# All token chunks routed ahead of the fused expert stage, whose freed memory holds more gather rows and a third weight pair; low halves later; tiles at 64 bytes

## The chip, the cores and the metric

One core of a Trainium2 chip runs the whole program. The metric is device time in microseconds (us) of one execution. PE is the matrix engine, DVE, ACT and POOL are the vector, scalar and GpSimd engines, SP is the engine whose queue issues most DMAs here. Each engine works through its own instructions in order; the program's order on each engine is set before it runs.

## What is computed

Two layers on x [1, 512, 1024] in fp32. A layer is `x + gate * mixer(h)` and then `x + gate * peer_ffn(h)`, each with `h = rms_norm(x) * (1 + scale) + shift`; shift, scale and gate come from `silu(c) @ w + b` (the modulation). The first layer's mixer is a gated linear recurrence (`rglru_mixer`), the second's is an attention with forget gates (`fox_mixer`). The part that the change is about is the ffn:

```python
def peer_ffn(h, q_w, subkey1, subkey2, expert_u, expert_v):   # per chunk xc of 128 tokens
    q = (xc @ q_w).reshape(128, 8, 2, 128)
    s1, s2 = q[:, :, 0] . subkey1, q[:, :, 1] . subkey2       # 128 keys each
    v1, i1 = top_k(s1, 16);  v2, i2 = top_k(s2, 16)
    top_s, top_c = top_k(v1[:, None] + v2[None, :], 16)       # per head
    expert = i1[top_c // 16] * 128 + i2[top_c % 16]           # of 16384
    g = softmax(top_s)
    act = gelu(expert_u[expert] . xc)
    return sum_k (g * act) * expert_v[expert]
```

## The kernel before

**Products.** A product of fp32 is three matmuls of rounded parts, hi x hi, lo x hi and hi x lo. `split` makes the parts: ACT copies the high half (L191), DVE subtracts it for the low half (L192). For weights these are `whi` and `wlo`. A `Stream` goes through a fixed plan of weight blocks of 512 KB; `fill` (L137) has SP load a pair of blocks (1 MB) into one of two `wraw` buffers and splits each block three ahead of its use. A buffer is free for the next load once DVE has subtracted its second block.

**The ffn (`peer`).** Tokens are four chunks of 128. The first three are computed densely: "expert" in the code is a group c of 128 experts (c = 0..127, those with the same first key), all 128 evaluated for 384 tokens, and weighted with a gate that is zero where the expert was not chosen. The fourth chunk is computed by gathering: for each of a token's 128 choices POOL fetches one row of u (later of v) per token by an indirect DMA of 128 rows, 512 KB (`fetch`, L700), into a ring of four `rows` buffers; DVE multiplies it with the token (L706) or adds it to the sum `accg` (L716).

Stages of `peer`: `queries` (products with the keys, top 16 on DVE); then a first-up stage, in which 56 groups (c < 56) are projected and their GELU stored to `ascr` in DRAM, with a `Background` that computes `route(0..2)` (which experts, from DVE operations on small tables) and `dense_gates(0..2)` (gate tables, stored to `gscr`) in small steps; then the fused stage, in the order c = 56..127 and then 0..55. I call its two parts A and B:

- A: `expert_in` projects the group (24 matmuls of 384 columns, L259 to L261), ACT takes the GELU (L751), DVE multiplies with the gate (L757, from `gtile`, loaded for eight groups at a time, L756), `split` makes `wh` and `wl`; `expert_out` then multiplies with v into six accumulators (18 matmuls of 512 columns, L769).
- B: the same, but the GELU comes back from `ascr` (L753, a ring of three `at2` buffers) instead of a projection.

During it `pump` runs the fourth chunk's generator `gathered` (its `route`, then 128 rows of u, then 128 of v) and some rows of modulation after it. A pump gives credits: 4.6 per group for the first eight, then 3.7 in A and 1.4 in B; a gathered row costs 1.2.

**Modulation rows (`mod_gen`).** Each row is a load of 512 KB by SP (L158) and a product on DVE (L160, L161). They are worked off as background elsewhere: eight rows of `l1_mix` at the end of the first mixer's output projection (the last argument of `lru`) and eight in the first ffn's fused stage (ring of four, that of the gathered rows); 12 in the attention's `during` (the 8 gates of `l1_mix` and 4 of `l1_ffn`'s 24 rows, one buffer) and the other 20 of `l1_ffn` after it.

The order on each engine comes from a scheduler that may move an instruction ahead of others of its engine; pools decide which load waits for which use.

Of the kernel before, what the change touches and what calls it, by code (L numbers as in the profile page):

```python
# [35 lines left out]
PUMP = (3.7, 1.4)  # L36
# [3 lines left out]
M1 = 8  # L40
M2 = 4
# [465 lines left out]
def peer(g, h, u, v, grow_fn, after, nd):  # L507
# [8 lines left out]
    with pool(tc, name="pk", bufs=1) as pk:  # L516
        hn = pk.tile([128, D], F32, name="hn")
        iota_f = iota_row(g, pk, 128, F16, "iota_f")
        iota_e = iota_f.rearrange("p (a b) -> p a b", b=8)
        vals = [pk.tile([128, TC, PH, TOPK], F32, name=f"vals{w}") for w in range(2)]  # L520
        idxs = [pk.tile([128, TC, PH, TOPK], U32, name=f"idxs{w}") for w in range(2)]
        def top16(val, idx, src, n):
            tk = pk.tile([128, 128], F32, name="tk", tag="tk", bufs=4)
# [54 lines left out]
        def route(t):  # L578

            v1, v2 = vals[0][:, t], vals[1][:, t]  # L580
            cand = pk.tile([128, PH, NCAND], F32, name="cand", tag="cand")
# [7 lines left out]
            top = pk.tile([128, PH, TOPK], F32, name="top", tag="top")  # L589
            pos = pk.tile([128, PH, TOPK], U32, name="pos", tag="pos")  # L590
# [11 lines left out]
            shp = [128, TOPK, HK]
            for q in range(2):
# [557 lines left out]
```

## Time and profile before

| | |
|---|---|
| median of 3 runs | 3401.5 us (3399.68 to 3401.56) |
| profiled execution, its own time | 3391.9 us, span 3390.2 us |
| mean granted TensorE clock | 0.973 |
| first ffn: fused A, fused B | 751 to 1393 us, 1393 to 1647 us |
| second ffn: fused A, fused B | 2485 to 3128 us, 3128 to 3385 us |
| DMA | 816.9 MB, 241 GB/s over the span |

The stages are windows of the trace: the first and last matmuls of L769 bound them, and A ends where the last projected group has been multiplied with v. Rows of a timeline read: start, duration, engine, line, operation, out<-in, and in brackets how long the engine had been idle before and what it waited for. Rows of the view of waits read: who waited for whom, us in total, times, longest.

### The profile page before, as it was taken

How to read it: one execution, taken by the hardware profiler on the slowest of the kernel's cores; microseconds unless marked ns; L12 is line 12 of the kernel's file. 1: busy time of each engine (PE TensorE's matmuls, PEld its weight loads, DVE VectorE, ACT ScalarE, POOL GpSimd, SP SyncE). 2: the span in 40 equal slices, each digit the busy share in tenths (PEclk: the TensorE clock that was granted, in tenths of full speed). 3: DMA queues.
4: the chain of work that ended last, by engine and by line, in shares of the span. 5: the costliest groups of instructions: out<-in, count | busy, mean ns of one | idle time of the engine just before them, and what ended most of it. 6: DMA issues, size and time to landing. Idle time of an engine off the chain costs nothing.

```text
span 3390.2 us, 44187 instructions
## 1 busy us (share of the span) xinstructions
PE 3158.9 (93%) x16256; PEld 2712.4 (80%) x16256; DVE 2647.0 (78%) x5245; ACT 1482.6 (44%) x2065; POOL 790.7 (23%) x672
## 2 busy tenths in 40 slices
PE   5987999999999999999999989999999999999999
PEld 4875889988888888777777767889988888887777
DVE  7867889876777787877679777799867777788775
ACT  4872237863333333333458723257843333332332
POOL 0000000003544454441000000000025454444430
PEclk9998999999999999999999989999999999999999
DMA  6445235778888889988441152336879888899994
GB/s 255 149 146 178 103 126 197 257 273 288 315 299 315 322 322 329 351 310 324 141 153 58 49 192 92 114 133 245 283 250 323 320 302 314 321 330 331 325 335 169
DMA packets 300762, 816.91 MB, mean 241 GB/s; under 512 B 24320, under 2 KB 153344, under 8 KB 272000
## 3 DMA queue, kind: packets, MB, share of 16 engines
q1 hardware_dynamic: 197312, 453.85, 38.6%
q0 software_dynamic: 75008, 269.00, 21.8%
q10 hardware_dynamic: 28224, 91.24, 6.9%
q8 instruction: 127, 2.08, 0.2%
q14 instruction: 91, 0.75, 0.1%
HBM read 733.00 MB, written 81.00 MB: 240 GB/s over the span
## 4 chain that ended last, share of the span: by engine, by line
issue 23%; PE 23%; DVE 19%; DMA 17%; POOL 10%; ACT 7%; SPq 0%; ACTq 0%; POOLq 0%; DVEq 0%
POOL rows L700 10%; DMA at<-ascr 6%; DMA rows<-in_l_v_dram,ei 6%; PE pacc L259 4%; DVE wlo L192 4%; PE pacc L260 4%; PE pacc L261 4%; PE vacc L769 2%; DVE accg L716 2%; PE gps L683 2%; DMA mw<-in_l_ffn_mw_dram 2%; DMA mw<-in_l_mix_mw_dram 1%; DVE mw L160 1%; ACT st L685 1%; ACT whi L191 1%
## 5 line engine op out<-in xcount | busy, mean ns | idle before, releaser
L191 ACT ACTIVATE whi<-wraw 128x1024 fp32r<-128x1024 f32 (+2 forms) x646 | 663.1, 1035 | 740.2 <-PE pacc L260 314.4
L261 PE MATMUL pacc<-hhi,wlo 128*128 128x384 f32 (+1 forms) x2632 | 935.4, 355 | 39.9 <-DVE wlo L192 39.9
L259 PE MATMUL pacc<-hhi,whi 128*128 128x384 f32 (+1 forms) x2632 | 930.6, 354 | 15.9 <-ACT at L751 14.4
L260 PE MATMUL pacc<-hlo,whi 128*128 128x384 f32 (+1 forms) x2632 | 930.0, 353 | 0.0
L192 DVE TENSOR_TENSOR wlo<-wraw,whi 128x1024 fp32r<-128x1024 f32 (+2 forms) x646 | 767.7, 1194 | 171.8 <-ACT whi L191 169.5
L769 PE MATMUL vacc<-whi,wh 128*128 128x512 f32 x1536 | 613.8, 400 | 23.6 <-ACT wh L191 23.4
L700 POOL DMA_INDIRECT rows<-in_l_u_dram,ei x256 | 370.1, 1446 | 1127.5 <-DMA wraw<-in_l_uT_dram 716.7
L769 PE MATMUL vacc<-wlo,wh 128*128 128x512 f32 x1536 | 612.9, 399 | 20.7 <-DVE wlo L192 20.5
L769 PE MATMUL vacc<-whi,wl 128*128 128x512 f32 x1536 | 612.1, 399 | 5.7 <-DVE wl L192 5.5
L261 PEld LDWEIGHTS pacc<-hhi,wlo 128*128 128x128 f32 x2632 | 502.7, 191 | 71.2 <-DVE wlo L192 49.8
L259 PEld LDWEIGHTS pacc<-hhi,whi 128*128 128x128 f32 x2632 | 503.1, 191 | 49.4 <-ACT at L751 16.6
L260 PEld LDWEIGHTS pacc<-hlo,whi 128*128 128x128 f32 x2632 | 502.2, 191 | 29.2 <-issue 2.4
L191 ACT ACTIVATE wh<-at 128x384 fp32r<-128x384 f32 x256 | 133.8, 524 | 806.4 <-DVE at L757 789.3
L700 POOL DMA_INDIRECT rows<-in_l_v_dram,ei x256 | 377.2, 1474 | 454.6 <-DVE accg L716 396.9
L706 DVE SCALAR_TENSOR_TENSOR rows<-rows,hn 128x1024 f32<-128x1024 f32 x256 | 304.6, 1221 | 130.3 <-DMA rows<-in_l_u_dram,ei 130.1
L769 PEld LDWEIGHTS vacc<-wlo,wh 128*128 128x128 f32 x1536 | 290.4, 189 | 94.6 <-DVE wlo L192 30.9
L769 PEld LDWEIGHTS vacc<-whi,wh 128*128 128x128 f32 x1536 | 290.7, 189 | 93.7 <-ACT wh L191 30.9
L769 PEld LDWEIGHTS vacc<-whi,wl 128*128 128x128 f32 x1536 | 290.7, 189 | 85.3 <-DVE wl L192 16.3
L716 DVE SCALAR_TENSOR_TENSOR accg<-rows,act,accg 128x1024 f32<-128x1024 f32 x254 | 325.5, 1282 | 41.0 <-DMA rows<-in_l_v_dram,ei 38.4
L757 DVE TENSOR_TENSOR at<-at,gtile 128x384 f32<-128x384 f32 x256 | 140.6, 553 | 108.4 <-DMA at<-ascr 105.9
L685 ACT ACTIVATE st<-gps 128x512 f32<-128x512 f32 x192 | 185.3, 1117 | 47.6 <-PE gps L683 45.2
L192 DVE TENSOR_TENSOR wl<-at,wh 128x384 fp32r<-128x384 f32 x256 | 141.3, 554 | 68.8 <-ACT wh L191 68.8
(266 smaller groups left out, 3229.5 us busy)
## 6 DMA issues: line engine op xcount, KB each, us to landing
wraw<-in_l_uT_dram SPq DMA_DIRECT2D x128, 1024.0 KB, 6.4
wraw<-in_l_v_dram SPq DMA_DIRECT2D x128, 1024.0 KB, 8.4
gscr<-st ACTq DMA_DIRECT2D x48, 1024.0 KB, 5.6
gtile<-gscr SPq DMA_DIRECT2D x32, 1536.0 KB, 12.3
mw<-in_l_mix_mw_dram SPq DMA_DIRECT2D x48, 512.0 KB, 6.4
mw<-in_l_ffn_mw_dram SPq DMA_DIRECT2D x48, 512.0 KB, 4.0
ascr<-at ACTq DMA_DIRECT2D x112, 192.0 KB, 4.1
at<-ascr SPq DMA_DIRECT2D x112, 192.0 KB, 5.2
```

Source lines behind the costliest of these rows:

```text
L191: g.nc.scalar.activation(hi, raw, AF.Copy)
L192: g.nc.vector.tensor_sub(lo, raw, hi)
L259: nc.tensor.matmul(ps, whi[:, k, :], hhi[:, k, :n], start=(k == 0), stop=False)
L260: nc.tensor.matmul(ps, whi[:, k, :], hlo[:, k, :n], start=False, stop=False)
L261: nc.tensor.matmul(ps, wlo[:, k, :], hhi[:, k, :n], start=False, stop=(k == KD - 1))
L683: T.matmul(gps[:, r, :], p2[:, tk_, :, :].rearrange("p a b -> p (a b)"), pg[i][:, :, tk_, :], start=(i == 0), stop=(i == 1))
L685: A.activation(st[:, :, q * 4:q * 4 + 4].rearrange("p e t -> p t e"), gps, AF.Copy, scale=1.0 / GSCALE)
L700: nc.gpsimd.indirect_dma_start(out=rows, out_offset=None, in_=src, in_offset=bass.IndirectOffsetOnAxis(ap=ei[:, j:j + 1], axis=0))
L706: V.scalar_tensor_tensor(r, r, 1.0, hn, op0=OP.mult, op1=OP.mult, accum_out=act[:, j:j + 1]))
L716: tc.keep_in_program_order(V.scalar_tensor_tensor(acc, r, w, acc, op0=OP.mult, op1=OP.add))
L757: V.tensor_tensor(at.rearrange("p (b t) -> p b t", t=16), at.rearrange("p (b t) -> p b t", t=16), env["gt"][:, :, c % 8, :], op=OP.mult)
L769: T.matmul(acc[t][d], x[:, ts], y[:, d, :], start=(i == 0 and x is wh and y is vh), stop=(i == PK - 1 and x is wl))
```

## The change

- `route` for the fourth chunk, with the indices `ei`, is computed at the end of the first-up stage's background instead of at the start of the fused stage. Routing's tiles lie in a pool `rt` of their own, which is closed before the fused stage.
- In the memory so freed: eight `rows` buffers instead of four, four `at2` buffers instead of three, and two more `wraw` buffers in the fused stage's pool `vw`, which take every third weight load (`g.stream.third`) until group PK - 16.
- `expert_in` leaves out the subtraction for `wl` and returns it, to be issued after the pump.
- The pump gives 3.5 in A and 1.3 in B, and the first eight groups are no exception.
- The first ffn's fused stage has all 16 first rows of `l1_mix` (ring of eight) and the end of the first mixer none; the attention's `during` has 16 first rows of `l1_ffn` beside the 8 gates, and 8 rows remain after it.
- `pad` puts small tiles into three pools, with a memset on POOL each. `hhi`, `hlo`, `whi`, `wlo`, `wraw` and what lies behind them begin at 0 modulo 64 bytes instead of 32; `wh`, `wl`, `gtile` and `rows` were at 0 and stay there; the attention's own tiles go from 0 to 32.

```diff
@@ -33,12 +33,11 @@
 NEG = -3.0e38
 NFIRST = 56
 NEARLY = 8
-PUMP = (3.7, 1.4)
+PUMP = (3.5, 1.3)
 GP = 4.0
 GSCALE = 32768.0
 M0 = 12
-M1 = 8
-M2 = 4
+M2 = 16
 MB = 1
 LP = 2.0
 
@@ -49,6 +48,11 @@
 
 def pool(tc, **kw):
     return tc.tile_pool(reuse_waits="tile", **kw)
+
+
+def pad(g, pool, size):
+
+    g.nc.gpsimd.memset(pool.tile([128, size // 4], F32, name="pad", bufs=1), 0.0)
 
 
 def bcast_rows(ap, n, length):
@@ -85,6 +89,7 @@
     nc.vector.memset(g.ones, 1.0)
     g.mhalf = g.const.tile([128, 1], F32, name="mhalf")
     nc.vector.memset(g.mhalf, -0.5)
+    pad(g, g.const, 32)
     g.order = range(TC)
 
 
@@ -124,7 +129,8 @@
         self.g, self.ahead = g, ahead
         self.blocks = [(i, b) for i in items for b in range(i[2])]
         self.raw, self.parts = None, []
-        self.n = 0
+        self.n = self.loads = 0
+        self.third = None
 
     def fill(self, last):
 
@@ -133,7 +139,9 @@
         while len(self.parts) <= last:
             (src, shape, n), b = self.blocks[len(self.parts)]
             if b == 0:
-                self.raw = g.wraw.tile([128, n, *shape], F32, name="wraw", tag="wraw")
+                self.loads += 1
+                src_pool = self.third if self.third and self.loads % 3 == 0 else g.wraw
+                self.raw = src_pool.tile([128, n, *shape], F32, name="wraw", tag="wraw")
                 nc.sync.dma_start(self.raw, src)
             raw = self.raw[:, b]
             hi = g.wsp.tile([128, *shape], F32R, name="whi", tag="whi")
@@ -515,12 +523,15 @@
     with pool(tc, name="pk", bufs=1) as pk:
         hn = pk.tile([128, D], F32, name="hn")
-        iota_f = iota_row(g, pk, 128, F16, "iota_f")
+        rguard = pool(tc, name="rt", bufs=1)
+        rt = rguard.__enter__()
+        pad(g, rt, 224)
+        iota_f = iota_row(g, rt, 128, F16, "iota_f")
...
-        thr = pk.tile([128, TOPK, HK], BF, name="thr")
+        thr = rt.tile([128, TOPK, HK], BF, name="thr")
...
-            cand = pk.tile([128, PH, NCAND], F32, name="cand", tag="cand")
+            cand = rt.tile([128, PH, NCAND], F32, name="cand", tag="cand")
...
-            gt = pk.tile([128, PH, TOPK], F32, name="gt", tag="gt_", bufs=3)
+            gt = (rt if t < nd else pk).tile([128, PH, TOPK], F32, name="gt", tag="gt_", bufs=3 if t < nd else 1)
...
             routes[t] = [*e, gt.rearrange("p a b -> p (a b)")]
+            if t >= nd:
+                ei = pk.tile([128, 128], I32, name="ei")
+                V.scalar_tensor_tensor(ei, e[0], float(PK), e[1], op0=OP.mult, op1=OP.add)
+                routes[t].append(ei)
             yield 0.6
@@ -688,10 +703,7 @@
 
         def gathered(t, out):
 
-            yield from route(t)
-            e1, e2, gt = routes[t]
-            ei = pk.tile([128, 128], I32, name="ei")
-            V.scalar_tensor_tensor(ei, e1, float(PK), e2, op0=OP.mult, op1=OP.add)
+            gt, ei = routes[t][2:]
             act = env["vw"].tile([128, 128], F32, name="act", tag="act", bufs=1)
             acc = env["vw"].tile([128, D], F32, name="accg", tag="accg", bufs=1)
 
@@ -729,15 +741,19 @@
             queries(pw, psum)
             natural(g, psum, h, TC - 1, hn)
             grow = grow_fn(psum)
-            bg = Background(*[route(t) for t in range(nd)], *[dense_gates(t, pu, pw, psum) for t in range(nd)])
+            bg = Background(*[route(t) for t in range(nd)], *[dense_gates(t, pu, pw, psum) for t in range(nd)],
+                            *[route(t) for t in range(nd, TC)])
             for c in range(NEARLY, NFIRST):
                 first_up(pw, psum, c)
                 bg.pump(GP)
             bg.finish()
+        rguard.__exit__(None, None, None)
         with pool(tc, name="vw", bufs=2) as vw, pool(tc, name="vps", bufs=1, space=PSUM) as psum:
-            gguard = pool(tc, name="gat", bufs=4)
+            gguard = pool(tc, name="gat", bufs=8)
             gat = gguard.__enter__()
             env["gat"], env["vw"] = gat, vw
+            pad(g, vw, 192)
+            g.stream.third = vw
             bg = Background(*late, *after(gat))
             acc = [[psum.tile([128, 512], F32, name=f"vacc{t}{d}") for d in range(2)] for t in range(nd)]
             order = [*range(NFIRST, PK), *range(NFIRST)]
@@ -746,7 +762,7 @@
             def expert_in(i):
 
                 c = order[i]
-                at = vw.tile([128, ND], F32, name="at2", tag="at2", bufs=3)
+                at = vw.tile([128, ND], F32, name="at2", tag="at2", bufs=4)
                 if c >= NFIRST:
                     A.activation(at, proj_t(g, psum, h, ND), AF.Gelu)
                 else:
@@ -758,8 +774,9 @@
                                 env["gt"][:, :, c % 8, :], op=OP.mult)
                 wh = vw.tile([128, ND], F32R, name="wh", tag="wh", bufs=5)
                 wl = vw.tile([128, ND], F32R, name="wl", tag="wl", bufs=5)
-                split(g, wh, wl, at)
+                A.activation(wh, at, AF.Copy)
                 ready[i] = (wh, wl)
+                return lambda: V.tensor_sub(wl, at, wh)
 
             def expert_out(i, t):
                 wh, wl, vh, vl = ready[i]
@@ -770,25 +787,25 @@
                                  stop=(i == PK - 1 and x is wl))
 
             def pump(i):
-                bg.pump(4.6 if i < 8 else PUMP[0] if order[i] >= NFIRST else PUMP[1])
-
-            expert_in(0)
-            expert_in(1)
+                bg.pump(PUMP[0] if order[i] >= NFIRST else PUMP[1])
+
+            expert_in(0)()
+            expert_in(1)()
             for i in range(0, PK - 4, 2):
+                if i == PK - 16:
+                    g.stream.third = None
                 ready[i] += g.stream.take()
                 ready[i + 1] += g.stream.take()
-                for t in range(nd):
-                    expert_out(i, t)
-                pump(i)
-                expert_in(i + 2)
-                for t in range(nd):
-                    expert_out(i + 1, t)
-                pump(i + 1)
-                expert_in(i + 3)
+                for j in (i, i + 1):
+                    for t in range(nd):
+                        expert_out(j, t)
+                    low = expert_in(j + 2)
+                    pump(j)
+                    low()
             bg.finish()
             gguard.__exit__(None, None, None)
             for i in (PK - 2, PK - 1):
-                expert_in(i)
+                expert_in(i)()
             last = range(PK - 4, PK)
             for i in last:
                 ready[i] += g.stream.take()
@@ -1057,8 +1074,8 @@
         with pool(tc, name="mw0", bufs=8) as mw:
             h = normed("l0_mix", mod=mod("l0_mix", mw, first, 8))
         lru(g, h, *arg("lru_", "conv", "bias", "lam"),
-            lambda p: (mod("l0_mix", p, gate, MB), mod("l0_ffn", p, first[:M0], MB)), grow("l0_mix"), lambda p: (mod("l0_ffn", p, (*first[M0:], *gate)), mod("l1_mix", p, first[:M1])))
-        peer(g, normed("l0_ffn"), flat("l0_u"), flat("l0_v"), grow("l0_ffn"), lambda p: (mod("l1_mix", p, first[M1:], 4),), 3)
+            lambda p: (mod("l0_mix", p, gate, MB), mod("l0_ffn", p, first[:M0], MB)), grow("l0_mix"), lambda p: (mod("l0_ffn", p, (*first[M0:], *gate)),))
+        peer(g, normed("l0_ffn"), flat("l0_u"), flat("l0_v"), grow("l0_ffn"), lambda p: (mod("l1_mix", p, first, 8),), 3)
         fox(g, normed("l1_mix"), *arg("fox_", "fb", "qg", "kg"), lambda p: (mod("l1_mix", p, gate, 1), mod("l1_ffn", p, first[:M2], 1)),
             grow("l1_mix"), lambda p: (mod("l1_ffn", p, (*first[M2:], *gate)),))
         peer(g, normed("l1_ffn"), flat("l1_u"), flat("l1_v"), grow("l1_ffn"), lambda p: (), 3)
```

Where it moves instructions. First DVE in part A of the first layer, once the rows flow (L757 gate multiplication, `wl` and `wlo` low halves, L706 gathered rows). Before:

```order
1273 L757 TENSOR_TENSOR at_7691<-at_7691,gtile 128x384
1274 L192 TENSOR_TENSOR wl<-at_7691,wh 128x384
1275 L192 TENSOR_TENSOR wlo<-wraw,whi 128x1024 x2
1276 L757 TENSOR_TENSOR at_7773<-at_7773,gtile 128x384
1277 L192 TENSOR_TENSOR wl<-at_7773,wh 128x384
1278 L706 SCALAR_TENSOR_TENSOR rows,act<-rows,hn 128x1024 x4
1279 L192 TENSOR_TENSOR wlo<-wraw,whi 128x1024 x2
1280 L757 TENSOR_TENSOR at_7839<-at_7839,gtile 128x384
1281 L192 TENSOR_TENSOR wl<-at_7839,wh 128x384
1282 L192 TENSOR_TENSOR wlo<-wraw,whi 128x1024
1283 L706 SCALAR_TENSOR_TENSOR rows,act<-rows,hn 128x1024 x4
```

The same place after (the lines are now L773, L718, L779 for `wl` and L200 for `wlo`):

```order
1247 L773 TENSOR_TENSOR at_7487<-at_7487,gtile 128x384
1248 L718 SCALAR_TENSOR_TENSOR rows,act<-rows,hn 128x1024 x3
1249 L779 TENSOR_TENSOR wl<-at_7487,wh 128x384
1250 L200 TENSOR_TENSOR wlo<-wraw,whi 128x1024 x2
1251 L773 TENSOR_TENSOR at_7552<-at_7552,gtile 128x384
1252 L718 SCALAR_TENSOR_TENSOR rows,act<-rows,hn 128x1024 x3
1253 L779 TENSOR_TENSOR wl<-at_7552,wh 128x384
1254 L200 TENSOR_TENSOR wlo<-wraw,whi 128x1024 x2
```

Each group now has the multiplication, three rows, `wl` and two `wlo`, where before groups without rows and groups with four alternated and `wl` stood right behind the multiplication.

DVE where the fused stage begins, before (the fold of the fourth chunk's route, L574, and its indices `ei`; behind them the first row):

```order
1245 L757 TENSOR_TENSOR at_7287<-at_7287,gtile 128x384
1246 L757 TENSOR_TENSOR at_7325<-at_7325,gtile 128x384
1247 L192 TENSOR_TENSOR wlo<-wraw,whi 128x1024
1248 L192 TENSOR_TENSOR wl<-at_7287,wh 128x384
1249 L192 TENSOR_TENSOR wl<-at_7325,wh 128x384
1250 L623 TENSOR_TENSOR ge<-j,col 128x1024
1251 L624 TENSOR_TENSOR ge<-ge,tab_7607 128x1024
1252 L574 TENSOR_TENSOR ge<-ge 128x512
1253 L574 TENSOR_TENSOR ge<-ge 128x256
1254 L574 TENSOR_TENSOR ge<-ge 128x128
1255 L576 TENSOR_TENSOR e_7513<-ge 128x64
1256 L694 SCALAR_TENSOR_TENSOR ei<-e_7512,e_7513 128x128
```

And after (L634, L635, L585, L587 are the same operations of the route, L648 `ei`):

```order
1234 L635 TENSOR_TENSOR ge<-ge,tab_7296 128x1024
1235 L200 TENSOR_TENSOR wlo<-wraw,whi 128x1024
1236 L585 TENSOR_TENSOR ge<-ge 128x512
1237 L585 TENSOR_TENSOR ge<-ge 128x256
1238 L585 TENSOR_TENSOR ge<-ge 128x128
1239 L587 TENSOR_TENSOR e_7236<-ge 128x64
1240 L648 SCALAR_TENSOR_TENSOR ei<-e_7235,e_7236 128x128
1241 L773 TENSOR_TENSOR at_7383<-at_7383,gtile 128x384
1242 L779 TENSOR_TENSOR wl<-at_7383,wh 128x384
```

The route's last steps and `ei` have moved ahead of the first multiplication; the route's earlier steps stood ahead of it in both.

SP's queue at the end of the first mixer, before (`lru_out` are its last weights, `qw` and `sk` the ffn's first, `gcol` belongs to the norm between):

```order
53 L137 DMA wraw<-in_l_qw_dram 128x2048
54 L158 DMA mw<-in_l_mix_mw_dram 128x1024 x2
55 L137 DMA wraw<-in_l_sk_dram 128x256
56 L155 DMA mod_b<-in_l_mix_mb_dram 128x24
57 L158 DMA mw<-in_l_mix_mw_dram 128x1024 x5
58 L204 DMA gcol<-in_l_ffn_g_dram 128x8
59 L137 DMA wraw<-in_l_sk_dram 128x256
60 L158 DMA mw<-in_l_mix_mw_dram 128x1024
```

After:

```order
53 L145 DMA wraw<-in_l_qw_dram 128x2048
54 L145 DMA wraw<-in_l_sk_dram 128x256
55 L163 DMA mod_b<-in_l_mix_mb_dram 128x24
56 L212 DMA gcol<-in_l_ffn_g_dram 128x8
57 L145 DMA wraw<-in_l_sk_dram 128x256
```

The eight loads of `l1_mix` rows are gone from there.

More of the change, by code (lines that the diff above doesn't have):

```diff
@@ L517, in peer @@
         hn = pk.tile([128, D], F32, name="hn")
-        iota_f = iota_row(g, pk, 128, F16, "iota_f")
+        rguard = pool(tc, name="rt", bufs=1)
+        rt = rguard.__enter__()
+        pad(g, rt, 224)
+        iota_f = iota_row(g, rt, 128, F16, "iota_f")
         iota_e = iota_f.rearrange("p (a b) -> p a b", b=8)
-        vals = [pk.tile([128, TC, PH, TOPK], F32, name=f"vals{w}") for w in range(2)]
-        idxs = [pk.tile([128, TC, PH, TOPK], U32, name=f"idxs{w}") for w in range(2)]
+        vals = [rt.tile([128, TC, PH, TOPK], F32, name=f"vals{w}") for w in range(2)]
+        idxs = [rt.tile([128, TC, PH, TOPK], U32, name=f"idxs{w}") for w in range(2)]
         def top16(val, idx, src, n):
-            tk = pk.tile([128, 128], F32, name="tk", tag="tk", bufs=4)
+            tk = rt.tile([128, 128], F32, name="tk", tag="tk", bufs=4)
             V.max(val[:, 0:8], src)
@@ L561, in peer @@
         HK = QH * TOPK
-        thr = pk.tile([128, TOPK, HK], BF, name="thr")
-        row = pk.tile([128, TOPK, HK], BF, name="rowlen")
-        col = pk.tile([128, TOPK, HK], BF, name="col")
+        thr = rt.tile([128, TOPK, HK], BF, name="thr")
+        row = rt.tile([128, TOPK, HK], BF, name="rowlen")
+        col = rt.tile([128, TOPK, HK], BF, name="col")
         for i in range(TOPK):
@@ L588, in route @@
             yield 1.5
-            top = pk.tile([128, PH, TOPK], F32, name="top", tag="top")
-            pos = pk.tile([128, PH, TOPK], U32, name="pos", tag="pos")
+            top = rt.tile([128, PH, TOPK], F32, name="top", tag="top")
+            pos = rt.tile([128, PH, TOPK], U32, name="pos", tag="pos")
             for hd in range(PH):
@@ L593, in route @@
                 yield 0.7
-            posb = pk.tile([128, PH * TOPK], BF, name="posb", tag="posb")
+            posb = rt.tile([128, PH * TOPK], BF, name="posb", tag="posb")
             V.tensor_copy(posb, pos.rearrange("p a b -> p (a b)"))
-            f1 = pk.tile([128, PH, TOPK], F32, name="f1", tag="f1")
+            f1 = rt.tile([128, PH, TOPK], F32, name="f1", tag="f1")
             V.tensor_copy(f1, idxs[0][:, t])
-            d1 = pk.tile([128, PH, TOPK], F32, name="d1", tag="d1")
+            d1 = rt.tile([128, PH, TOPK], F32, name="d1", tag="d1")
             V.tensor_copy(d1[:, :, 0:1], f1[:, :, 0:1])
             V.tensor_sub(d1[:, :, 1:], f1[:, :, 1:], f1[:, :, :-1])
-            e = [pk.tile([128, PH * TOPK], F32, name=f"e{w}", tag=f"e{w}", bufs=3) for w in range(2)]
+            e = [rt.tile([128, PH * TOPK], F32, name=f"e{w}", tag=f"e{w}", bufs=3) for w in range(2)]
             shp = [128, TOPK, HK]
@@ L607, in route @@
                 for w, src in enumerate((d1[:, hs], idxs[1][:, t, hs])):
-                    x = pk.tile(shp, BF, name=f"tab{w}", tag=f"tab{w}")
+                    x = rt.tile(shp, BF, name=f"tab{w}", tag=f"tab{w}")
                     A.activation(x.rearrange("p r (h k) -> p r h k", h=QH),
@@ L611, in route @@
                     tab.append(x)
-                ge = pk.tile(shp, BF, name="ge", tag="ge")
-                ge2 = pk.tile(shp, BF, name="ge2", tag="ge2")
+                ge = rt.tile(shp, BF, name="ge", tag="ge")
+                ge2 = rt.tile(shp, BF, name="ge2", tag="ge2")
                 ps_ = posb[:, ks]
@@ L619, in route @@
                 yield 2.6
-                j = pk.tile([128, HK], BF, name="j", tag="j")
+                j = rt.tile([128, HK], BF, name="j", tag="j")
                 fold(ge2, j)
```

2 lines of the change are left out of this document (1 added, 1 removed).

## The prediction, made before the changed kernel had run

> **What bounds the kernel now.** I read the page's busy shares first, then cut the span by stage, then asked in each stage what every engine waits for, and last how fast an undisturbed expert runs.
>
> ```profile
> PE 3158.9 (93%) x16256; PEld 2712.4 (80%) x16256; DVE 2647.0 (78%) x5245; ACT 1482.6 (44%) x2065; POOL 790.7 (23%) x672
> core 0: us, PE busy (x) PEld busy (x) DVE busy (x) ACT busy (x) POOL busy (x), PEclk, DMA share, GB/s
> 751.00:1393.00 642.00, 613.66 (x2976) 543.93 (x2975) 491.39 (x634) 206.47 (x286) 306.61 (x213) 0.98 0.86 311
> 1393.00:1647.00 254.00, 240.73 (x1009) 188.53 (x1008) 192.53 (x263) 85.60 (x114) 69.75 (x46) 0.99 0.87 312
> 2485.00:3128.00 643.00, 610.68 (x2978) 540.73 (x2977) 492.20 (x636) 207.15 (x286) 304.08 (x213) 0.98 0.87 311
> 3128.00:3385.00 257.00, 241.36 (x1008) 189.49 (x1006) 179.66 (x221) 79.95 (x107) 68.18 (x44) 0.99 0.79 283
> ```
>
> The four windows are the two fused stages, each cut into A (72 experts projected on the spot) and B (56 experts read back from `ascr`). They hold 1796 of the span's 3390.2 us, so the price of one expert decides. A quiet expert is read from three GELUs of stage A and eighteen output products of stage B:
>
> ```profile
> 793.64 0.47 ACT L751 ACTIVATE at<-pacc 128x384 f32<-128x384 f32 x1
> ...
> 818.78 0.47 ACT L751 ACTIVATE at<-pacc 128x384 f32<-128x384 f32 x1
> 1427.20 0.40 PE L769 MATMUL vacc<-whi,wh 128*128 128x512 f32 x1
> ...
> 1431.40 0.40 PE L769 MATMUL vacc<-whi,wh 128*128 128x512 f32 x1
> 2014.82 0.39 PE L299 MATMUL oacc<-whi,yhi 128*128 128x512 f32 x1
> ...
> 2018.90 0.39 PE L299 MATMUL oacc<-whi,yhi 128*128 128x512 f32 x1
> ```
>
> Between the GELUs lie three experts: 25.14 / 3 = 8.38 us. Between the two `vacc` rows lie 18 matmuls, all of one expert in B: 4.20 us, 233 ns each. The floors are 72 x 8.38 = 603 and 56 x 4.20 = 235 us; measured are 642, 254, 643 and 257. So 39, 19, 40 and 22 us are lost, 120 in all. What PE, DVE and ACT waited for in the first A, and the later B's waits:
>
> ```profile
> PE pacc L261 <- DVE wlo L192: 17.4, 11, 2.6
> PE vacc L769 <- ACT wh L191: 8.5, 8, 2.3
> DVE rows L706 <- DMA rows<-in_l_u_dram,ei: 65.9, 32, 4.3
> DVE wl L192 <- ACT wh L191: 33.1, 56, 0.6
> DVE wlo L192 <- ACT whi L191: 31.7, 35, 4.0
> DVE accg L716 <- DMA rows<-in_l_v_dram,ei: 16.1, 13, 2.5
> ACT whi L191 <- DMA wraw<-in_l_v_dram: 11.8, 5, 3.5
> ACT whi L191 <- DMA wraw<-in_l_uT_dram: 11.0, 3, 4.4
> SPq L137 <- DVE wlo L192: 551.8, 69, 12.4
> PE vacc L769 <- DVE wlo L192: 10.3, 6, 4.1
> DVE at L757 <- DMA at<-ascr: 60.0, 29, 8.2
> ACT whi L191 <- DMA wraw<-in_l_v_dram: 55.9, 15, 8.2
> SPq L753 <- DVE wl L192: 97.9, 33, 8.6
> ```
>
> In A the DVE is 491.4 us busy and 146.8 waiting by these four rows: 638 of 642. It has no slack, though PE is the busier engine: it works in order, so whatever it waits for delays the weights' low halves (`wlo`), for which PE then waits. It waits longest for gathered rows (82 us), since only four can be in flight; SP's next weight load waits for `wlo` all the while.
>
> **The change, part by part.**
>
> *Stage A: eight rows, low half later, lower pump.* Rows per expert go from 3.7/1.2 = 3.08 to 3.5/1.2 = 2.92. A row occupies DVE 1.15 us from start to start:
>
> ```profile
> 1055.31 1.22 DVE L706 SCALAR_TENSOR_TENSOR rows<-rows,hn 128x1024 f32<-128x1024 f32 x1
> ...
> 1056.45 1.22 DVE L706 SCALAR_TENSOR_TENSOR rows<-rows,hn 128x1024 f32<-128x1024 f32 x1
> ```
>
> So 72 x 0.16 x 1.15 = 13 us of DVE work leave. The 33.1 us of waiting for `wh` go: rows now stand between the gate multiplication and `wl`, and three rows outlast ACT's copy (longest wait 0.6). The rows' 82 us: twice the buffers give a gather some 8 / 2.92 = 2.7 experts or 23 us to land instead of 11; the longest wait is 4.3, so most should go. What is left is 491 - 13 plus perhaps 45 of waits, 523 against 603: PE binds, DVE has about 80 us of cover. Bounds for the excess of 39: 0 (every stall goes) to 39 (the stalls come from shared transfers, not from too few buffers). Near the short end, since DVE's own rows name the wait: I keep 13, because half-clock stretches and some late loads will stay. **-26 in each A.**
>
> *Transfers.* An expert of A moves u and v (1.05 MB), 2.92 rows (1.53) and an eighth of a gate tile (0.20): 2.78 MB, 331 GB/s at 8.38 us. B's 0.52 + 0.20 + 0.20 + 0.57 = 1.49 MB ask 354 at 4.20. The windows moved 311 at 0.86 busy, so 360 at full share by the same rate. A has room; B is at the edge.
>
> *Stage B: fourth `at2`, third weight pair.* `at` is late 60.0 us in 29 times (2.1 each), its load being held by `wl` on SP's queue. One more buffer issues it an expert (4.2 us) earlier, less the 1.2 that the later `wl` gives back: most of it goes. v is late 55.9 in 15 times (3.7 each); a further pair issues every third load far ahead and gives the others the time of about one load more. By transfers at 360 GB/s the second B needs 56 x 1.49 / 360 = 232 us, so its 235 is within reach; I say 245: **-12**. The first B now also carries all 16 rows of `l1_mix` (8 before): (83.4 + 4.2) MB / 360 = 243, and six or so of them remain for the end; I say 248: **-6**. Bounds for both together: 0 to -41.
>
> *The 64-byte tiles.* The only instructions whose operands differ in offset (the stationary `wh` at 0 modulo 64 bytes, the moving `whi` at 32) are L769's; they start 233 ns apart. `oacc`, of the same shape with both at 32, starts 4.08 / 18 = 227 apart. If the mismatch is the reason, all at 0 saves 6.6 ns x 18 = 0.12 us an expert: 8.6 in each A, up to 6.7 in each B, 30 at most and 0 at least. Nothing else that I see separates the two groups, so I take the nearest row: 17 for both A, and 4 for the second B, the first being held by transfers: **-21**. In the Trainium skill, "TensorE: Matmul & The Clock Gate" (section "Wait — 56ns, not 53.3ns?") gives warm back-to-back matmuls a start-to-start of N / 2.4 GHz plus 2.5 ns, 215.7 ns for 512 columns, with no part for addresses. By it the pads would bring nothing and the sum would be 21 us poorer; neither 233 nor 227 obeys it, so it does not decide.
>
> *Rows of modulation, moved.* The end of the first mixer:
>
> ```profile
> 293.00:310.00 17.00, 3.78 (x16) 3.14 (x16) 11.87 (x29) 5.57 (x10) 2.17 (x3) 0.50 0.91 319
> 305.66 2.71 PE L217 MATMUL xt<-ident,xn 128*128 128x128 f32 x11 [17.36 <-DVE xn L215]
> 299.24 1.22 DVE L160 SCALAR_TENSOR_TENSOR mw<-mw,sc 128x1024 f32<-128x1024 f32 x1 [2.05 <-DMA mw<-in_l_mix_mw_dram]
> ```
>
> PE waits 17.4 us for DVE's `xn`, while DVE works off eight rows of `l1_mix`. They leave SP's queue and DVE's order there: 8 x 1.22 = 10 us of work and several waits for their loads like the 2.05. Bounds -5 (only half of that work was in PE's way) to -17 (the whole gap); the gap at the second mixer's end, next, is 9.6 in all, so **-11**. At the end of the second mixer PE waits similarly (5.68 and 3.91 in the rows below), with 20 rows of which 12 leave: **-5** (0 to -10).
>
> ```profile
> 2028.23 0.48 PE L217 MATMUL xt<-ident,xn 128*128 128x128 f32 x1 [5.68 <-DVE gt L270]
> 2032.62 1.97 PE L217 MATMUL xt<-ident,xn 128*128 128x128 f32 x8 [3.91 <-DVE xn L215]
> 1700.00:1800.00 100.00, 99.69 (x455) 73.76 (x454) 78.13 (x157) 61.02 (x109) 9.92 (x20) 1.00 0.40 135
> 1800.00:1900.00 100.00, 99.11 (x503) 74.74 (x502) 88.41 (x204) 80.31 (x163) 7.01 (x14) 1.00 0.16 55
> ```
>
> Those 12 go into the attention's first stretch, with one buffer each waiting for the last: 12 x 1.22 = 15 us of DVE in windows where DVE is 78 and 88% busy and PE 99%. Mostly beside PE; **+3** (0 to +10).
>
> *Start of the fused stage.* Before, the gather's route ends behind the first two gate multiplications:
>
> ```profile
> 739.23 0.38 SPq L137 DMA_DIRECT2D wraw<-in_l_v_dram  x1
> 739.78 6.03 SPq L756 DMA_DIRECT2D gtile<-gscr  x2
> 748.92 0.56 DVE L757 TENSOR_TENSOR at<-at,gtile 128x384 f32<-128x384 f32 x1
> 753.18 0.68 DVE L623 TENSOR_TENSOR ge<-j,col 128x1024 bf16<-128x1024 bf16 x1
> 755.92 0.29 DVE L694 SCALAR_TENSOR_TENSOR ei<-e,e 128x128 int32<-128x128 f32 x1
> 757.13 2.01 POOL L700 DMA_INDIRECT rows<-in_l_u_dram,ei  x1 [280.47 <-DMA wraw<-in_l_uT_dram]
> ```
>
> Now all of it, up to `ei`, stands ahead of the first multiplication, and the gate tile lies in routing's memory: its load can only issue when DVE has read the last of it. Route's remainder behind the two multiplications was 753.2 to 756.2, 3 us; a gate tile needs some 9 us from issue (739.8 to 748.9). So the first multiplication comes 3 to 10 us later, and PE, which has only two projections ahead, waits that long; **+5** per layer, +10. The gathers start some us sooner, which pays nothing while DVE has room. The pads themselves are five small memsets on POOL, idle for 280 us there: 0.
>
> **Sum.** -52 (A) - 18 (B) - 21 (pads) - 11 - 5 + 3 + 10 = -94. The profiled execution took 3391.9 us beside its span of 3390.2, the median of the runs is 3401.5, 9.6 higher; carried over, 3401.5 - 94 = **3308**.
>
> **Rivals.**
> 1. *The pads do nothing* (the 233 ns come from something else in L769): 3308 + 21 = 3329. For it: the projections have both operands at 32 and suffer nothing, so a bare offset of 32 is harmless.
> 2. *Transfers are the limit already.* At 0.86 busy with slices of unequal load, eight gathers in flight delay the weights as much as they help DVE; A keeps two thirds of its excess and B all. Then -26 - 16 + 3 + 10, with half of the pads (-10): -39, 3363. For it: 0.86 to 0.87 busy in three of the four windows, whether DVE has row work or less. Against: DVE's waits are short (65.9 us in 32) and A asks for 331 of 360.
> 3. *Slower:* a burst of freed row buffers puts up to eight gathers (4.2 MB, 12 us at 360) ahead of a weight pair on the shared engines. A pair serves two experts, 16.8 us; if it lands more than 0.65 us late per expert over the 144 experts of A, the 94 are eaten, and at 1.0 us late the time is 3401 + 50 = 3451. The pairs' own lead grows by a buffer, which speaks against it; DMA at 0.86 speaks for it.
> 4. *The stage start costs 15 a layer,* since the gate tile queues behind weight loads on SP: 3328 with the pads.
>
> **How the numbers follow.** Forecast 0.42 (3290 to 3335); rival 1 0.22; rival 2 0.17; rival 4 0.06, all faster: 0.87. Rival 3 beyond 0.65 us 0.08; about at 0.65, no change, 0.05. About 0.2% (7 us) is what a measurement of this kernel can tell from no change. The range for 8 in 10 goes from 3270 (both B at their floor, all stalls of A gone) to 3385 (rival 2 without pads and with a slow start); it leaves rival 3 above.
>
> **What would show it.** GELUs of A 8.25 us apart (8.38 if the pads fail); windows of A near 608, of B near 248 and 245; `rows` no longer the first of DVE's waits; `at<-ascr` under 20 us; PE's 17.4 us gap near 6; the first multiplication later than `ei`. I am wrong if A stays above 630 with DVE idle on `rows`, or if ACT waits for `wraw` in A for more than the 23 us of now.

## The result and the profile after

The changed kernel takes 3302.4 us in the median (3299.5 to 3307.8, 4 runs) against 3401.5 before (4 runs on that chip): the ratio is 0.9706, 95% interval 0.9685 to 0.9727, 2.9% faster. 3308 was forecast. The profiled execution has a span of 3299.1 us, 91.1 less than before. One run of one experiment, with the rows ahead of the multiplication, had a granted clock of 0.84 and took 3462 us; it is left out of that median. The page's busy shares and the four windows of the fused stages (columns as before the change):

```profile
PE 3117.9 (95%) x16256; PEld 2713.4 (82%) x16256; DVE 2625.0 (80%) x5245; ACT 1497.5 (45%) x2065; POOL 719.8 (22%) x677
747.00:1341.00 594.00, 592.44 (x2977) 537.84 (x2976) 475.25 (x623) 215.94 (x287) 266.93 (x209) 1.00 0.94 340
1341.00:1598.00 257.00, 238.72 (x1008) 192.62 (x1008) 202.12 (x277) 82.20 (x111) 65.69 (x43) 0.97 0.88 318
2440.00:3034.00 594.00, 592.44 (x2977) 537.87 (x2976) 475.81 (x623) 216.49 (x286) 262.24 (x206) 1.00 0.94 335
3034.00:3293.00 259.00, 238.31 (x1007) 191.70 (x1008) 181.68 (x226) 78.99 (x107) 66.26 (x43) 0.97 0.78 275
```

Both A went from 642 to 594 us, PE is busy for all of it and its clock is full. Both B became 2.6 us longer (253.9 to 256.6, 256.5 to 259.2, from first and last L769 matmul). Cut by matmuls, the span's 91 us are:

| stretch, us | before | after | change | forecast |
|---|---|---|---|---|
| both A | 641.8 + 642.2 | 594.3 + 594.3 | -95.4 | -69 with the pads |
| both B | 253.9 + 256.5 | 256.6 + 259.2 | +5.4 | -22 with the pads |
| first mixer's last product to the ffn's gate row | 181.6 | 174.4 | -7.2 | -11 |
| the same after the second mixer | 182.2 | 169.7 | -12.5 | -5 |
| first ffn's end to the second mixer's last product | 374.3 | 380.7 | +6.4 | +3 |
| gate row to the first product with v, both | 281.9 + 281.8 | 282.4 + 291.6 | +10.3 | +10 |

The rest (+2) lies ahead of the first mixer's last product, which comes at 286.9 to 289.9 us in the changed kernel and the experiments, so it tells nothing. The waits in the first A (three rows), then DVE's wait for `at` in the first and the second B, and ACT's for v in both:

```profile
PE vacc L786 <- ACT wh L777: 4.9, 2, 3.4
DVE wlo L200 <- ACT whi L199: 118.1, 72, 4.4
ACT whi L199 <- PE pacc L268: 206.3, 70, 3.0
DVE at L773 <- DMA at<-ascr: 47.0, 14, 8.5
DVE at L773 <- DMA at<-ascr: 62.1, 19, 8.7
ACT whi L199 <- DMA wraw<-in_l_v_dram: 11.4, 3, 6.6
ACT whi L199 <- DMA wraw<-in_l_v_dram: 0.5, 1, 0.5
```

In A the chain of waits has turned round: DVE waits for ACT's `whi`, ACT for PE to be done with the old ones, and PE, after 4.9 us at the start of the stage, for nobody. In B v is hardly late any more (52.4 and 55.9 us before), but `at` is as late as it was (41.6 and 60.0), in fewer and longer waits (longest 8.5 and 8.7, 6.0 and 8.2 before).

The two places where a fused stage begins, and the first mixer's end:

```profile
745.48 0.56 DVE L773 TENSOR_TENSOR at<-at,gtile 128x384 f32<-128x384 f32 x1 [6.39 <-DMA gtile<-gscr]
2438.39 1.03 DVE L773 TENSOR_TENSOR at<-at,gtile 128x384 f32<-128x384 f32 x2 [14.61 <-DMA gtile<-gscr]
295.07 3.61 PE L225 MATMUL xt<-ident,xn 128*128 128x128 f32 x16 [4.82 <-DVE xn L223]
```

The first gate tile is what DVE waits for, as forecast; in the second ffn DVE could start 16.3 us after its issue at 2422.1, in the first 9.1 after 736.4. PE's gap of 17.36 at the first mixer's end is 4.82.

### The profile page after: what moved, and what is told of

Read it like the earlier page. It is cut to its first block, busy times and chain, and to the rows that moved or that the text cites. A ratio compares the mean times of both kernels' runs of the same rounds, so it can differ in the third digit from the quotient of the medians.

```text
span 3299.1 us, 44224 instructions
## 1 busy us (share of the span) xinstructions
PE 3117.9 (95%) x16256; PEld 2713.4 (82%) x16256; DVE 2625.0 (80%) x5245; ACT 1497.5 (45%) x2065; POOL 719.8 (22%) x677
## 4 chain that ended last, share of the span: by engine, by line
PE 60%; DVE 19%; DMA 10%; ACT 6%; issue 4%; POOL 0%; SPq 0%; ACTq 0%; DVEq 0%; POOLq 0%
PE vacc L786 22%; PE pacc L269 10%; PE pacc L268 10%; PE pacc L267 10%; DMA at<-ascr 5%; DVE wlo L200 4%; PE gps L698 2%; DVE accg L728 2%; DVE mw L168 1%; DMA mw<-in_l_ffn_mw_dram 1%; ACT st L700 1%; ACT whi L199 1%; DMA wraw<-in_l_qw_dram 1%; DVE tk L537 1%; DMA mw<-in_l_mix_mw_dram 1%
## 5 line engine op out<-in xcount | busy, mean ns | idle before, releaser
L200 DVE TENSOR_TENSOR wlo<-wraw,whi 128x1024 fp32r<-128x1024 f32 (+2 forms) x646 | 770.4, 1194 | 324.5 <-ACT whi L199 323.8
L786 PE MATMUL vacc<-wlo,wh 128*128 128x512 f32 x1536 | 610.4, 397 | 33.2 <-DVE wlo L200 33.1
L786 PE MATMUL vacc<-whi,wl 128*128 128x512 f32 x1536 | 603.5, 394 | 2.0 <-DVE wl L779 2.0
L712 POOL DMA_INDIRECT rows<-in_l_u_dram,ei x256 | 333.5, 1303 | 1092.9 <-issue 483.7
L712 POOL DMA_INDIRECT rows<-in_l_v_dram,ei x256 | 340.8, 1331 | 465.0 <-DVE accg L728 434.2
L786 PEld LDWEIGHTS vacc<-whi,wh 128*128 128x128 f32 x1536 | 292.1, 190 | 84.9 <-ACT wh L777 25.7
L718 DVE SCALAR_TENSOR_TENSOR rows<-rows,hn 128x1024 f32<-128x1024 f32 x256 | 299.8, 1220 | 0.0
L773 DVE TENSOR_TENSOR at<-at,gtile 128x384 f32<-128x384 f32 x256 | 141.2, 553 | 130.2 <-DMA at<-ascr 109.1
L168 DVE SCALAR_TENSOR_TENSOR mw<-mw,sc 128x1024 f32<-128x1024 f32 x96 | 116.7, 1220 | 41.4 <-DMA mw<-in_l_ffn_mw_dram 23.1
```

Source lines behind the costliest of these rows:

```text
L168: nc.vector.scalar_tensor_tensor(wf, wf, 1.0, g.sc, op0=OP.mult, op1=OP.mult, accum_out=dot)
L200: g.nc.vector.tensor_sub(lo, raw, hi)
L712: nc.gpsimd.indirect_dma_start(out=rows, out_offset=None, in_=src, in_offset=bass.IndirectOffsetOnAxis(ap=ei[:, j:j + 1], axis=0))
L718: V.scalar_tensor_tensor(r, r, 1.0, hn, op0=OP.mult, op1=OP.mult, accum_out=act[:, j:j + 1]))
L773: V.tensor_tensor(at.rearrange("p (b t) -> p b t", t=16), at.rearrange("p (b t) -> p b t", t=16), env["gt"][:, :, c % 8, :], op=OP.mult)
L786: T.matmul(acc[t][d], x[:, ts], y[:, d, :], start=(i == 0 and x is wh and y is vh), stop=(i == PK - 1 and x is wl))
```

## The experiments

All but three (the two with the old loop, and the last) alter the changed kernel in one respect. Times are medians, ratios are against the kernel before on the same chip. Lengths of A and B are of one profiled execution each, between the starts of matmuls.

**No pads.**

```diff
-    pad(g, g.const, 32)
-        pad(g, rt, 224)
-            pad(g, vw, 192)
```

> The changed kernel without its three pads, so that hhi, whi and wraw begin at 32 modulo 64 bytes again and wh at 0. Theory 'equal offsets': L769's successor starts every 233 ns again instead of 226 to 231, a quiet expert of A costs 8.38 us instead of 8.25 and A lasts about 603 instead of 594 us (it has no stall left, so it shows the floor); B gets up to 6 us longer each; total 3302 + 18 to 30 = 3320 to 3332. Rival 'not the pads' (the shorter spacing comes from the regular order or the quieter queues): spacing stays at 226 to 231, total 3302 within 7.

3318.5 us, 0.9760 (0.9744 to 0.9776). But A stayed at 594.2 and 593.6, and the spacing of the products with v (L769 before, L783 here) fell to 227 ns. The numbers fit neither theory: without pads `wh` and `wl` also lie at 32, since routing's pool moved them, so nothing is mixed. B holds 16 of the 19 us by which the span grew: 269.3 and 262.5.

**Mixed offsets**, the true test: weights at 32, `wh` and `wl` at 0.

```diff
-    pad(g, g.const, 32)
-            pad(g, vw, 192)
+            pad(g, vw, 224)
```

> The changed kernel with whi and hhi at 32 modulo 64 bytes and wh, wl at 0, as before the change (the first pad left out, the third longer by 32 bytes); nothing else moves. In the run without pads all of them lay at 32, so it did not test this mixture. Theory 'unequal offsets slow L769's matmuls': spacing 233 ns, quiet expert in A 8.38 us, A 603 us each, quiet expert in B 4.20; total 3302 + 18 to 30. Rival 'the spacing of 233 had another reason': A stays 594, quiet B 4.08 to 4.13, total within 12 of 3302.

3315.7 us, 0.9741 (0.9721 to 0.9762); A 599.2 and 598.7, B 262.7 and 263.6, a quiet expert of B 4.20 again. The spacing is the theory's, the total is short of its 3320 to 3332. The timelines of PE in a quiet stretch of B, with 18 matmuls between the two rows of each pair; first mixed, then all at 32 (no pads), then all at 0 (the changed kernel):

```profile
1462.18 0.39 PE L785 MATMUL vacc<-whi,wh 128*128 128x512 f32 x1
...
1466.38 0.39 PE L785 MATMUL vacc<-whi,wh 128*128 128x512 f32 x1
```

```profile
1462.27 0.39 PE L783 MATMUL vacc<-whi,wh 128*128 128x512 f32 x1
...
1466.35 0.39 PE L783 MATMUL vacc<-whi,wh 128*128 128x512 f32 x1
```

```profile
1462.10 0.39 PE L786 MATMUL vacc<-whi,wh 128*128 128x512 f32 x1
...
1466.22 0.39 PE L786 MATMUL vacc<-whi,wh 128*128 128x512 f32 x1
```

4.20, 4.08 and 4.12 us: 233, 227 and 229 ns a matmul. Unequal offsets cost 5 us in each A (599 against 594), little more than half of the 8.6 that I had taken. That A of 599 has no stalls left, so it is what the old spacing allows: of the 95 us that both A gained, 10 are the offsets and 85 the stalls.

**Four rows buffers.**

```diff
-            gguard = pool(tc, name="gat", bufs=8)
+            gguard = pool(tc, name="gat", bufs=4)
```

(and 4 in `mod`'s ring for the same tag.)

> The changed kernel with four rows buffers instead of eight, all else as it is. Theory 'too few gathers in flight made DVE wait': DVE's first wait in A is for rows again with 60 us or more, and A lasts 605 to 640 instead of 594 us each; total 3325 to 3395. Rival 'order and low half did it': DVE waits for rows under 20 us, A stays within 5 of 594, total within 7 of 3302. For B: if eight gathers in flight delay the loads of at there, four make B shorter than 257 and 259 us.

3309.7 us, 0.9743 (0.9724 to 0.9761); A 593.1 and 593.2. This refutes, for the new loop, that A needs more than four gathers in flight: DVE's waits for rows in the first A are only

```profile
DVE rows L718 <- DMA rows<-in_l_u_dram,ei: 5.0, 10, 1.1
```

B did not get shorter either (260.2 and 264.0).

**Low half at once**, ahead of the rows.

```diff
-                    low = expert_in(j + 2)
-                    pump(j)
-                    low()
+                    expert_in(j + 2)()
+                    pump(j)
```

> The changed kernel with the low half wl subtracted right behind the gate multiplication, ahead of the rows. DVE waits 0.6 us per expert for wh again, 33 to 42 us per A. Theory 'DVE has slack now' (475 us busy of 594): A stays within 3 of 594 us, total within 7 of 3302. Rival 'the wait for wh was part of the bound': A 10 to 40 us longer each, total 3320 to 3380.

3285.2 us, 0.9664 (0.9648 to 0.9680): faster than the changed kernel, by 14 us if the ratios are compared and by 17 if the medians are, and below both ranges expected. A is 591.5 and 592.0 though DVE waits 41 us for `wh` again; B is 250.3 and 255.2, with 33.1 and 53.8 us of waiting for `at` (47.0 and 62.1 with the low half later). An `at2` buffer is free only when `wl` has been subtracted, so an earlier low half frees it earlier.

**Two weight pairs.**

```diff
-            g.stream.third = vw
```

> The changed kernel without the third weight pair (all loads through the two wraw buffers). Theory 'the pair only helps B, where ACT waited 56 us for v before': ACT waits 30 to 55 us for v in each B, B gets 3 to 12 us longer each, A stays within 6 of 594; total 3305 to 3330. Rival 'A needs it, since DMA is 0.94 busy there': PE waits for wlo in A again (10 to 25 us), A 605 to 625; total 3325 to 3365.

3311.4 us, 0.9742 (0.9726 to 0.9759); A 594.4 twice, B 263.4 and 260.5. ACT waits 25.7 us for v in the first A, yet PE loses nothing there. In B its waits for v are

```profile
ACT whi L199 <- DMA wraw<-in_l_v_dram: 75.5, 17, 8.2
ACT whi L199 <- DMA wraw<-in_l_v_dram: 70.5, 17, 10.4
```

against 11.4 and 0.5 with the third pair, and yet B is only 6.8 and 1.3 us longer.

**Modulation rows where they were** (`M1`, `M2` and the two calls as before, ring of eight).

> The changed kernel with the modulation rows where they were before (eight of l1_mix after the first mixer, twelve of l1_ffn after the second). By the two traces the move gave 7 us between the first mixer's last product and the next ffn's gate row (181.6 to 174.4) and 12.5 at the second mixer (182.2 to 169.7), and cost 6.4 between the first ffn's end and the attention's end (374.3 to 380.7). Theory 'the rows are the cause of all three': +7, +12.5, -6.4, and the first B 0 to 8 us shorter with 4.2 MB less; total 3307 to 3316. Rival 'the attention got longer by its tiles at 32 bytes instead of 0': the 380.7 stay, total 3313 to 3322.

3317.6 us, 0.9742 (0.9723 to 0.9761). The stretches behind the mixers are 185.1 and 180.5 us again, the attention 375.6, so the rows are the cause of all three: their move is worth -10.7, -10.8 and +5.1. The first B, with eight rows less to work off, is no shorter (258.0 against 256.6). PE's gap at the first mixer's end is back:

```profile
304.80 1.54 PE L226 MATMUL xt<-ident,xn 128*128 128x128 f32 x6 [15.86 <-DVE xn L224]
```

**Rows ahead of the multiplication**, the old order (with the low half at once), with the new buffers and pump.

```diff
-                    low = expert_in(j + 2)
-                    pump(j)
-                    low()
+                    pump(j)
+                    expert_in(j + 2)()
```

> The changed kernel with the pump ahead of expert_in, as before, and the low half at once: DVE gets the three rows of an expert ahead of its gate multiplication, between the two wlo. Eight buffers, third pair and pump values stay. Theory 'the order rows, then multiplication made PE wait': wlo and wh come late again, PE waits 10 to 30 us per A, A 604 to 625; total 3325 to 3365. Rival 'slack of DVE is enough (475 of 594 us), order does not matter': A within 4 of 594, total 3285 to 3310, with B like that of the run with the low half first.

3303.9 us, 0.9714 (0.9686 to 0.9742); A 594.2 and 592.6, so order alone does not matter to A. B is 262.0 and 255.1; the kernel with the low half at once, which differs from this one in the order alone, has 250.3 and 255.2, so the order matters to the first B.

**The whole old loop**: old order, 3.7 and 1.4 with 4.6 at first, four rows, two pairs.

```diff
-PUMP = (3.5, 1.3)
+PUMP = (3.7, 1.4)
-            bg.pump(PUMP[0] if order[i] >= NFIRST else PUMP[1])
+            bg.pump(4.6 if i < 8 else PUMP[0] if order[i] >= NFIRST else PUMP[1])
...
```

> The changed kernel with the whole loop of before: pump ahead of expert_in, low half at once, 3.7 and 1.4 credits (4.6 for the first eight), four rows buffers, two weight pairs. Routing ahead, four at2 buffers, offsets and the modulation rows stay as changed. Theory 'loop and buffers together made A's stalls': A 620 to 640, with DVE waiting for rows 50 us or more; total 3350 to 3395. Rival 'the route and its memory made them' (routing in the fused stage shifted all rows): A within 6 of 594, total 3295 to 3320.

3404.0 us, 1.0003 (0.9990 to 1.0016): the whole gain is gone. A is 648.9 and 663.9, B 244.1 and 244.3, with 227 rows fetched by the end of each A (213 and 212 in the kernel before, where the route used part of the pump's credits). So A's gain rests on the new loop with its pump values, the eight buffers and the third pair; routing ahead, the fourth `at2` buffer, the offsets and the moved modulation rows, which this kernel keeps, bring nothing in sum without them.

**The old loop with eight rows buffers.**

> The kernel with the old loop (pump ahead of expert_in, 3.7 and 1.4 with 4.6 at first, two weight pairs), whose A took 649 and 664 us, with one thing given back: eight rows buffers instead of four. DVE's order is the same in both. Theory 'too few gathers in flight, where DVE takes four rows at a time': DVE's wait for rows (53 us per A) goes, A 594 to 610 each; total 3265 to 3310. Rival 'the old order or the two pairs make the stalls': A stays over 630, total 3350 to 3400.

3331.0 us, 0.9780 (0.9731 to 0.9829); A 633.3 and 632.0. The waits of the first A, with four rows and then with eight:

```profile
DVE rows L718 <- DMA rows<-in_l_u_dram,ei: 53.4, 27, 3.7
DVE accg L728 <- DMA rows<-in_l_v_dram,ei: 13.1, 16, 1.9
ACT whi L199 <- DMA wraw<-in_l_uT_dram: 36.3, 6, 10.4
ACT whi L199 <- DMA wraw<-in_l_v_dram: 8.8, 5, 3.2
```

```profile
ACT whi L199 <- DMA wraw<-in_l_uT_dram: 44.8, 9, 13.1
ACT whi L199 <- DMA wraw<-in_l_v_dram: 36.7, 13, 7.3
```

The waits for rows are all gone, as the theory said, and A is still 38 us over the changed kernel's: the lateness moved to the weights, 45 to 82 us. The profiled execution (3349 us) was the slowest of the four, so part of the 38 may be its own; what of the rest is the second pair, the old order or the 4.6 of the first eight was not taken apart.

**Old pump values alone** (`PUMP = (3.7, 1.4)`).

> The changed kernel with the pump values of before, 3.7 and 1.4 (without the 4.6 of the first eight); order, eight buffers, third pair stay. An expert of A then gathers 3.08 rows instead of 2.92, 2.86 MB, at 8.25 us 347 GB/s instead of 337. Theory 'the lower pump keeps A under what the transfers give': A 610 to 640, B shorter by 3 to 8 (six rows fewer a layer, 13 in the two): total 3325 to 3370. Rival 'order and buffers give slack for 3.08 rows too': A 594 to 600 each, B 4 to 8 shorter; total 3290 to 3305.

3268.8 us, 0.9604 (0.9588 to 0.9621): the fastest of all, 34 us under the changed kernel, its interval lies below, and so does the time below both ranges expected. Windows:

```profile
748.00:1342.00 594.00, 592.74 (x2976) 538.11 (x2976) 489.01 (x633) 215.98 (x287) 280.28 (x219) 0.99 0.96 348
1342.00:1586.00 244.00, 233.01 (x1006) 188.08 (x1007) 189.92 (x264) 82.06 (x111) 50.31 (x32) 1.00 0.86 313
3028.00:3271.00 243.00, 230.30 (x985) 186.29 (x983) 165.71 (x212) 77.88 (x105) 46.41 (x29) 0.98 0.73 262
```

A fetches eleven rows more in the same 594 us, at 348 GB/s; B has eleven fewer and is 12.5 and 16.3 us shorter. The lower pump of the change was a loss.

**Gate tiles from ACT's queue** (`nc.scalar.dma_start`). SP's timeline in B of the changed kernel had shown an issue that takes 7.65 us behind a gate tile:

```profile
1428.59 0.37 SPq L772 DMA_DIRECT2D gtile<-gscr  x1
1431.42 7.65 SPq L769 DMA_DIRECT2D at<-ascr  x1
1439.13 0.77 SPq L145 DMA_DIRECT2D wraw<-in_l_v_dram  x1
```

> The changed kernel with the gate tiles loaded from ACT's queue instead of SP's. In B SP's next issue behind a gate tile took 4 to 8 us (7.65 at 1431.4), and the loads of at stand behind it. Theory 'the gate tile blocks SP's queue and so at': DVE's wait for at falls from 47 and 62 us to under 25, each B 8 to 16 us shorter, and the start of the second ffn's fused stage gets shorter as well; total 3270 to 3290. Rival 'at comes late because it is asked for late and lands in 6 to 9 us among the other transfers': the waits stay above 40, B within 6 of 257 and 259, total 3295 to 3312; ACT may lose a few us where its own queue blocks.

3309.8 us, 0.9736 (0.9717 to 0.9754); B 263.3 and 259.1, the waits for `at` 47.9 and 58.1, although SP's longest issue in B is now 1.70 us. The long issue is not what makes `at` late.

**Three together**: no pads, low half at once, 3.7 and 1.4.

> The changed kernel without pads (all operands of L769 at 32 modulo 64 bytes, spacing 227 ns), with the low half at once and with the pump values 3.7 and 1.4. If the three parts add up: A 588 to 593 each (4.08 instead of 4.12 for the products with v), B 236 to 243 each with fewer rows left and at freed earlier; total 3240 to 3262. Rival 'they share one gain' (both the higher pump and the earlier low half relieve B of the same waits): B 243 to 250, total 3258 to 3275.

3296.2 us, 0.9678 (0.9631 to 0.9725), a miss: A 592.0 and 591.8, but B 263.7 and 252.5, where the pump alone had 244 and 243. All three kernels with the weights at 32 have a B that is longer than that of their neighbour at 0, but not in one place: here the first seven experts of B take 45.0 and 42.1 us (33.3 and 33.5 with the pump alone), while without pads the third to fifth seven lose most. In the first B (1345 to 1560 us) the loads of v land in 7.7 us and those of `at` in 7.0 without pads, in 7.9 and 7.0 in the mixed kernel, and in 6.9 and 6.3 in the changed one; why is open.

## Why the prediction was right, and where its steps failed

**A: right in place and sign, too small, and for a reason that the runs do not carry.** That DVE had no slack was right: it was busy or waiting for 638 of 642 us, and now PE hardly waits. That its order made PE wait is not shown, since the old order costs the new loop nothing in A. The step "the rows' 82 us: twice the buffers" failed: four buffers in the new loop leave 5.0 us of them, and eight in the old loop remove them and leave A at 633. Each of rows, low half, third pair, order and pump can be taken back alone at no cost to A (591.5 to 594.4); all together cost 55 and 70 us. So the change has several remedies for one shortage, and any one of them may be missing; eight buffers alone are not enough. Which smaller set is enough stays open. The excess that I kept, 13 us, was 0.

**Pads: mechanism right, size half in A.** The mixture costs, 233 against 227 to 229 ns; the pads are one way out of it, and leaving all at 32 is another. My 8.6 us per A was 5: with equal offsets three GELUs of A lie 24.92 us apart, 8.31 an expert, where I had expected 8.25. In B the mixed kernel is 6.1 and 4.4 us longer; I had taken 0 and 4.

**Pump: the sign of a term was wrong.** I counted the lower pump as 12 rows and 13 us less DVE work in A. DVE worked off 209 rows in the first A before and 207 after, since the old pump's credits had to pay for the route as well. A did not need less either: at the old values it takes eleven rows more at no cost, and B is 29 us shorter in both together.

**B: failed.** "One more buffer issues it an expert earlier, less the 1.2 that the later `wl` gives back" is the step. `at` takes 6.3 us to land instead of 5.2 (medians of all loads), and DVE's wait for it stayed. With the low half at once that wait falls from 47.0 and 62.1 us to 33.1 and 53.8, and B by 6.3 and 4.0. SP's own waits for `wl` do not show this: in the first B they are 71.7 us before, 83.3 after, and 102.4 with the low half at once, where B is shorter. No run takes the fourth buffer alone away, so its worth is not shown.

The larger part is the rows, which I had priced in B by their bytes alone. In the changed kernel 24 of the 26 us that the first B loses against quiet experts fall ahead of the 169th us, and all of the second's ahead of the 202nd, while the last row is used at 183 and 187 us. Seven experts there take up to 37.5 and 40.8 us, and 28.8, 4.12 each, in most of what follows. With the old pump the last row is used at 117 and 118 us, and that shortens B more than the low half does. Whether a row delays B by its transfer or by its 1.28 us on DVE was not separated; the eight modulation rows added behind the gathered ones cost B nothing (258.0 without them).

Nor was 360 GB/s the edge: in the second B of the changed kernel the 40 slices read

```profile
GB/s 398 396 413 413 401 380 406 192 340 370 365 410 187 273 388 386 271 319 296 317 181 383 294 223 276 273 203 397 253 211 140 253 207 155 112 183 164 0 80 82
```

Eight of the first dozen slices, while rows are gathered, have 380 to 413, and all of the last dozen, when that is over, under 260. The mean of a window, divided by its busy share, was no capacity. The third pair did what was forecast to v (its lateness went from 55.9 to 0.5, and is 70.5 without the pair), but it bought only 8 us in both B, since `at` was late as well.

**Modulation rows.** Forecast -11, -5 and +3; undoing the move alone gives -10.7, -10.8 and +5.1. The second was mis-sized: I bounded it by the two gaps of the norm, 9.6 us, and took half. From the mixer's last product to the gate row, PE's idle time fell by 8.5 us; the other 4 are work of PE that went faster, at a granted clock of 0.96 instead of 0.92:

```profile
2021.40:2203.60 182.20, 163.80 (x818) 138.81 (x817) 140.66 (x610) 52.96 (x72) 6.38 (x52) 0.92 0.33 117
1978.30:2148.00 169.70, 159.83 (x819) 135.12 (x818) 130.47 (x588) 53.12 (x72) 6.95 (x53) 0.96 0.29 104
```

**Start of the stage.** +5 each was forecast, +0.5 and +9.8 came, by the wait that was named. The +0.5 was luck: in the other experiments with this start the first stretch is 283 to 295 us, where it was 282.4 here. In the second ffn eight gathers (2424.6 to 2434) were issued while the gate tile was on its way, but with four `rows` buffers, so four gathers, DVE still starts 15.3 us after the tile's issue, and 14.9 in the first ffn. Their number is therefore not the cause; what makes the tile late stays open.

Of the rivals, the pads doing nothing is refuted by the mixed kernel; transfers as A's limit by 594 us at 348 GB/s; late weights in A by PE's 4.9 us of waiting. A start that costs 15 a layer came nearest in the second ffn, with 9.8. A's surplus of 26 and B's shortfall of 27 cancelled; that the total came so close to 3308 was luck.

## What to carry to other kernels

When a resource waits for several things in turn, taking away the one with the longest total says little about the gain: undo each part of a fix alone, and then all together. Work that can be done in either of two stages belongs where it delays nothing: here eleven rows moved from B to A were free in A and shortened B by 12.5 and 16.3 us. A buffer added to a ring counts from the operation that frees it; in this case doing that operation earlier shortened both B, and the worth of the buffer itself was not measured.

## What the runs showed of the hardware that was not expected

The time from start to start of 512-column fp32 matmuls changed with the offsets of the two operands modulo 64 bytes: 233 ns for 32 with 0, 227 for 32 with 32, 229 for 0 with 0 (mixed, no pads, changed kernel). In the Trainium skill, "SBUF — State Buffer" (Operand start alignment) treats start addresses as a matter of legality and says that its runs timed nothing; here a legal address costs 2 to 3%. In the first B a packet of 512 bytes, the pieces of the gate tiles, took 27.5 ns in the mean into tiles at 0 modulo 64 and 29.9 without pads, where the tiles lie at 32. An issue on SP behind such a load of 1.5 MB took 7.65 us where others take 0.32; with the gate tiles on ACT's queue none on SP took over 1.70. And 348 GB/s were held for 594 us (old pump values).
